# Row scales of two norms by way of DRAM, and the MLP norm's squares taken on token-major rows

## The chip, the core and the metric

One core of a Trainium2 chip runs the whole kernel. The engines are TensorE (PE, whose weight loads are listed as PEld), VectorE (DVE), ScalarE (ACT), GpSimd (POOL) and SyncE (SP, which here only issues transfers). Each engine takes its instructions in order and waits on semaphores of the others. The metric is the time of one execution in microseconds on the device.

## The reference

One layer of a streaming encoder, in float32, on 512 tokens of width 1024. Cut to what matters here:

```
def rmsnorm(x, g):
    return x * rsqrt(mean(x * x, axis=-1) + EPS) * g

hn   = rmsnorm(h, norm_mix_g);  proj = hn @ w_in        # 8 groups of columns
h    = h + concat(fox_attention, hgrn2) @ w_out
h    = h + memory_cross_attention(rmsnorm(h, norm_x_g), rmsnorm(mem, norm_mem_g))
u    = rmsnorm(h, norm_ff_g) @ w1                       # 1024 -> 4096
h    = h + square(relu(u)) @ w2                         # 4096 -> 1024
return rmsnorm(h, final_norm_g)
```

A norm's scale, one number per token, can be left out ahead of the product and put onto the product's result. The first norm's four gate columns (gf0 to gf3), its gq columns and the MLP's u are scaled this way.

## The kernel before, in words

Activations lie feature-major in SBUF for the projections: 128 features on the partitions, 512 tokens in the free dimension, eight such chunks for 1024 features. Every float32 operand is split into a high and a low part, and a product of a [128 x 512] result tile over eight chunks is 24 matmuls: high by high, high by low and low by high (lines 236 to 238, `gemm_fm`). Weights come from DRAM into raw tiles (`wr2a` and so on, 512 KB each, issued by SP), ACT copies out the high part (`wh2a`, line 171), DVE subtracts to get the low part (`wl2a`, line 175); the matmuls with the low part wait for DVE.

A feature-major result has tokens in the free dimension, so the scale must lie there too: a tile `rbc` of [128 x 512] which holds the 512 scales on every partition. The scale itself is computed with tokens on the partitions, four columns for the four blocks of 128 tokens: a [128 x 4] tile (`r0`, later `r2`). To get from the one to the other, PE multiplies each column, repeated 128 times, with the identity: four float32 matmuls of 128 columns into a PSUM bank (lines 516 and 1507), and DVE copies the bank to SBUF (lines 518 and 1508). Readers of `rbc` are the gates `sg` (line 540), the gq and fox tiles, and the MLP's `ur = max(u, 0) * rbc2` (line 1305).

Stage 1 begins the kernel. `ms0` (mean squares of x) is ready after four row sums; POOL makes r0 (lines 357 and 360). PE works on gf2 then: its broadcast is put after 15 of gf2's 24 matmuls. Chunks of x that are later needed again are parked: copied from PSUM to `xT` (`x_park`, lines 422 and 424) and written by POOL to `xTd` in DRAM. The copies also free PSUM banks, gf3's and gq's among them. In this stretch the order on ACT and DVE is the order of the code.

Stage 2 is the passage from cross-attention to the MLP. The residual's eight chunks (`xw`, in `residual`) leave PE; POOL squares each chunk and adds it into `ssq` (15 instructions of 128 x 512, lines 1073 to 1077); after the first MLP product u000, PE sums `ssq` over the partitions with a column of ones (`pm`, line 1087), DVE scales it (line 1089), POOL makes r2 and PE broadcasts it (line 1507) after u001. Meanwhile the chunks are transposed to token-major (`to_tok`), so that the rows `acc` (four tiles of [128 tokens x 1024]) collect the MLP's output. The MLP runs in eight groups of 512 hidden features: four products u(g)(j)(i) a group into two PSUM banks of the pool `mm`; `ur` and its square free the bank; then `mlp_down` multiplies in a scheme of seven products ("1", "2", "6", "5", "7", "3", "4") with banks U, Y and V. Product "6" goes into the same U bank as "1", after DVE has added "1" into `acc` (line 1335).

The raw tiles of the down weights (`wq`) are loaded by SP, and the scheme's sums of weights are made by transfers that add (`add_weights`, line 1245, issued by POOL): first from DRAM, two a group; then, once product "2" has its split, inside SBUF (`wq<-wq`: a1 += a2, then b1 += a1). The weights of product "6" are a1 after that add.

Outside stage 1 and the last product, a scheduler sets the order on each engine from the order of the code and its own estimates.

Of the kernel before, what the change touches and what calls it, by code (L numbers as in the profile page):

```python
# [42 lines left out]
def emit(  # L43
# [310 lines left out]
    def rstd_of(ms, n, name, r=None):  # L354
# [5 lines left out]
        gp.tensor_tensor(r, e, mhalf[:, 0:n], op=ALU.pow)  # L360
        return r

    def norm_rows(t, name):
        ms = sm(2, name + "m")
        for i in range(2):
            junk = t2(f"{name}j{i}")
            ac.activation(junk, t[:, i * S : (i + 1) * S], AF.Square, scale=1.0 / 32.0, accum_out=ms[:, i : i + 1])
        ve.tensor_tensor(ms[:, 0:1], ms[:, 0:1], ms[:, 1:2], ALU.add)
        r = rstd_of(ms[:, 0:1], 1, name + "r")
        ve.tensor_scalar(t, t, r, None, op0=ALU.mult)  # L370
# [67 lines left out]
    with tc.manual_schedule(engines={mybir.EngineType.Activation, mybir.EngineType.DVE}):  # L438
        ve.tensor_copy(g_mix, gmp)
        x_T(0)  # L440
        warm = mm("warm2")
        for _ in range(WARM2):
            te.matmul(warm, zero[:, 0:P], zero, start=True, stop=True)
        first[0]("v")
        x_hi(0)
        x_lo(0)
        first[0]("l")
        wt0 = stream[0]
        state["used"] = 1
        gfps = [mm(f"gf{i}") for i in range(2)]  # L450

        def first_rows(w, a, start):
            for i in range(2):
                te.matmul(gfps[i], chunk(w, 0, slice(i * P, (i + 1) * P)), a[:, 0, :], start=start, stop=False)

        first_rows(wt0[0], hn_hi, True)
        x_T(1)
        x_hi(1)
        x_lo(1)
        first_rows(wt0[0], hn_lo, False)  # L460
        first_rows(wt0[1], hn_hi, False)
        gfg = [gemm_fm(gfps[i], wt0, i * P, hn_hi, hn_lo, order=range(1, KC), begun=True) for i in range(2)]
        second = []

        def l_soft():

            gps = sc("gps", (33,))
            te.transpose(gps, rows, ident[0:33, 0:33])
            ve.tensor_copy(gv, gps)
            ve.tensor_tensor(lmx, gv[:, 25:29], gv[:, 29:33], ALU.max)  # L470
            ve.tensor_tensor(le, gv[:, 25:33].rearrange("p (r k) -> p r k", r=2), lmx.unsqueeze(1).to_broadcast([P, 2, 4]), ALU.subtract)
            ac.activation(le, le, AF.Exp)
            ve.tensor_tensor(lden, le[:, 0, :], le[:, 1, :], ALU.add)
            ve.reciprocal(lden, lden)
            ve.tensor_tensor(lb, le[:, 0, :], lden, ALU.mult)
            ve.tensor_scalar(oml, lb, -1.0, 1.0, op0=ALU.mult, op1=ALU.add)

        jobs = (
            (first[1],),
            (lambda: x_park(0), lambda: x_park(1), first[2]),  # L480
            (first[3], lambda: second.extend(load_next())),
            (lambda: x_sq(0), lambda: x_park(3)),
            (lambda: x_park(2), lambda: second[0]("h"), lambda: x_sq(2)),
            (lambda: x_sq(1), lambda: second[0]("l"), lambda: x_sq(3)),
            (lambda: second[1]("hl"), l_soft),
            (),
        )
        for c in range(KC):
            for g in gfg if c else ():
                next(g)  # L490
            if c + 2 < KC:
                x_T(c + 2)
                x_hi(c + 2)
                x_lo(c + 2)
            for job in jobs[c]:
                job()
        for g in gfg:
            assert next(g, None) is None
        x_park(7)

        wt1 = stream[1]
        state["used"] = 2
        third = load_next()
        gfps.append(mm("gf2"))
        gf2 = gemm_fm(gfps[2], wt1, 0, hn_hi, hn_lo)
        for _ in range(GF):
            next(gf2)
        r0 = cp.tile([P, NT], F32, name="r0")
        rstd_of(ms0, NT, "r0", r0)

        fb = cp.tile([P, FH], F32, name="fb")
        gp.tensor_copy(fb[:, 0:NT], r0)
        gp.dma_start(fb, fox_f_bias[0].partition_broadcast(P))
        pb = sc("rbc")
        for tb in range(NT):
            te.matmul(pb[:, tb * P : (tb + 1) * P], r0[:, tb : tb + 1].to_broadcast([P, P]), ident, start=True, stop=True)
        rbc = cp.tile([P, S], F32, name="rbc")
        ve.tensor_copy(rbc, pb)
        run_now(gf2)
        gfps.append(mm("gf3"))  # L520
        gf3 = gemm_fm(gfps[3], wt1, P, hn_hi, hn_lo)


        Fg, Mv, Sa, Ag = [], [], [], []
        for hp in range(2):
            Fg.append(s4([2, S], f"F{hp}"))
            Mv.append(s4([2, S], f"mov{hp}"))
            Sa.append(s4([2, S], f"sta{hp}"))

        def kt_(h):  # L530
            return (Sa, Mv)[h % 2][h // 2][:, h % 2, :]

        def qt_(h):
            return (Mv, Sa)[h % 2][h // 2][:, h % 2, :]


        sg = [t2(f"sg{h}") for h in range(4)]

        def gate(h):
            ve.tensor_tensor(sg[h], gfps[h], rbc, ALU.mult)  # L540
            ac.activation(sg[h], sg[h], AF.Sigmoid)

        def forget(h):
            F_ = Fg[h // 2][:, h % 2, :]
            ac.activation(F_, sg[h], AF.Identity, scale=oml[:, h : h + 1], bias=lb[:, h : h + 1])
            ac.activation(kt_(h), F_, AF.Identity, scale=-1.0, bias=1.0)

        x_park(4)
        x_park(6)
        gate(0)  # L550
        gate(1)
        x_park(5)
        third[0]()
        third[1]()
        run_now(gf3)
        gate(2)
        for h in range(3):
            forget(h)
# [3 lines left out]
    for hp in range(2):  # L562
        wt = next_panel()
        for j in range(2):
            h = 2 * hp + j
            ps = mm(f"gq{h}")
            run_now(gemm_fm(ps, wt, j * P, hn_hi, hn_lo))
            ve.tensor_tensor(qt_(h), ps, rbc, ALU.mult)
            ac.activation(qt_(h), qt_(h), AF.Silu)
# [476 lines left out]
    def residual(src_hi, src_lo, g, dst_hi, dst_lo, name, ssq, order, nlast, after=None):  # L1046
# [16 lines left out]
        def rest():  # L1063
            for c in range(KC):
                if c not in gens:
                    open_(c)
                yield from gens[c]
                hc = hTc(c)
                ve.tensor_tensor(hc, hc, ps_[c], ALU.add)  # L1069
                ac.activation(dst_hi[:, c, :], hc, AF.Identity, scale=g[:, c : c + 1])  # L1070
                ve.scalar_tensor_tensor(dst_lo[:, c, :], hc, g[:, c : c + 1], f(dst_hi[:, c, :]), op0=ALU.mult, op1=ALU.subtract)
                if c == 0:
                    gp.tensor_tensor(ssq, hc, hc, op=ALU.mult)
                else:
                    sq = t2(f"{name}sq{c}")
                    gp.tensor_tensor(sq, hc, hc, op=ALU.mult)
                    gp.tensor_tensor(ssq, ssq, sq, op=ALU.add)
                if after is not None and c in (2, 4, 6):
                    after(c - 2)
                    after(c - 1)  # L1080
# [85 lines left out]
    def to_tok(c):  # L1166
# [3 lines left out]
        for tb in range(NT):  # L1170
            d, s_ = acc[tb][:, c * P : (c + 1) * P], ps[:, tb * P : (tb + 1) * P]
            if tb % 2 == 0:
                ac.activation(d, s_, AF.Copy)
            else:
                ve.tensor_copy(d, s_)

    fill.add(x_proj(1), "xq1")
    fill.run(2.0)
    for h in range(4):
        if 0 < h < 3:  # L1180
            fill.add(x_proj(h + 1), f"xq{h + 1}")
        elif h == 3:
            x2_hi, x2_lo = act_tile("x2_hi"), act_tile("x2_lo")
            ssq2 = t2("ssq2")
            early, rest = residual(o_hi, o_lo, g_ff, x2_hi, x2_lo, "xw", ssq2, range(KC), 2, to_tok)
            fill.add(early())
        x_scores(h, 0)
        fill.run(X1)
# [107 lines left out]

    def mlp_up(g, j, wt):
        for i in range(2):
            ps = mm(f"u{g}{j}{i}")
            run_now(gemm_fm(ps, wt, i * P, x2_hi, x2_lo))  # L1300
            yield g, j, i, ps

# [171 lines left out]
    def mlp_up_group(g):  # L1474
        for j in range(2):
            if g < 2:
                wt = next_panel()
                if (g, j) == (0, 0):
                    down_raws(0)
                elif (g, j) == (1, 1):  # L1480
                    for _ in range(2):
                        unit_q.popleft()[1]()
# [14 lines left out]
    rbc2 = rbc  # L1497
    ups = mlp_up_group(0)
    up0 = next(ups)
    ms2 = mean_sq(ssq2, "pm2")  # L1500
    r2 = rstd_of(ms2, NT, "r2")
    to_tok(KC - 2)
    to_tok(KC - 1)
    up1 = next(ups)
    pb = tr("rbc2")
    for tb in range(NT):
        te.matmul(pb[:, tb * P : (tb + 1) * P], r2[:, tb : tb + 1].to_broadcast([P, P]), ident, start=True, stop=True)
    ve.tensor_copy(rbc2, pb)
    square(*up0)
    square(*up1)  # L1510
    for up in ups:
        square(*up)
    hidden_sums(0)
    for name in PRODUCTS:
# [42 lines left out]
```

## Time and profile before

| | |
|---|---|
| time, median of 3 runs | 769.85 us (768.88 to 769.93) |
| the profiled execution | 769.28 us |
| its span, first to last instruction | 767.5 us |
| PE busy | 759.0 us (99%) |
| DVE, ACT, POOL busy | 523.7 (68%), 368.7 (48%), 190.5 us (25%) |
| mean granted TensorE clock | 0.998 |
| DMA | 103.03 MB, mean 134 GB/s |

The span is 1.8 us less than the profiled execution's time; what lies around the span is the start and the end of a launch. Times on a timeline count from the span's start. A matmul's row gives its start and a duration that is modelled and reaches into the next; the distance from one start to the next is what it takes of PE. A timeline row may cover several like instructions in a row (x2, x4, x8); a float32 matmul stands as two. "Landing" is the time from a transfer's issue to its completion.

### The profile page before, as it was taken

The numbers are of one execution on the slowest core, as the hardware profiler recorded it, in microseconds if no ns is written. First come the engines' busy times: TensorE is split into PE (matmuls) and PEld (weight loads), VectorE is DVE, ScalarE is ACT, GpSimd is POOL, SyncE is SP. The second block draws the span as 40 slices with busy tenths as digits, with TensorE's granted clock in tenths as the row PEclk, the third lists the DMA queues.
The fourth block names the chain that finished last, engine by engine and source line by source line (L and its number), as shares of the span: only waits on it lengthen the run. The fifth ranks groups of instructions, "written<-read, shape, count | busy, mean of one in ns | idle before, by whom it ended". The sixth has DMA issues, their size and how long they took to land.

```text
span 767.5 us, 11244 instructions
## 1 busy us (share of the span) xinstructions
PE 759.0 (99%) x4229; PEld 646.0 (84%) x4229; DVE 523.7 (68%) x849; ACT 368.7 (48%) x620; POOL 190.5 (25%) x264
## 2 busy tenths in 40 slices
PE   9999999999999999999999999999999999999996
PEld 6889888998889988888888888888888888888885
DVE  5747765576787656555548556949596868777696
ACT  5655456665666433344444244435353535342553
POOL 7207432423432025310016510101001010101123
PEclk9999999999999999999999999999999999999999
DMA  8543332232543442231113596565748475757602
GB/s 247 192 136 108 90 84 56 80 114 57 185 149 134 163 139 83 85 100 64 56 56 108 204 262 139 146 158 175 180 149 200 139 174 161 192 137 218 138 1 109
DMA packets 79831, 103.03 MB, mean 134 GB/s; under 512 B 4593, under 2 KB 58394, under 8 KB 79778
## 3 DMA queue, kind: packets, MB, share of 16 engines
q1 hardware_dynamic: 70226, 76.61, 31.1%
q0 software_dynamic: 8960, 24.67, 15.3%
q10 hardware_dynamic: 592, 1.05, 0.4%
q8 instruction: 33, 0.54, 0.3%
q14 instruction: 20, 0.16, 0.1%
HBM read 89.71 MB, written 4.21 MB: 122 GB/s over the span
## 4 chain that ended last, share of the span: by engine, by line
PE 98%; DVE 1%; ACT 1%; POOL 0%; issue 0%; DVEq 0%; ACTq 0%
PE u L238 8%; PE u L236 8%; PE u L237 8%; PE U L1371 4%; PE U L1369 4%; PE U L1370 4%; PE xq L236 2%; PE xq L237 2%; PE xw L236 2%; PE xq L238 2%; PE xw L237 2%; PE xw L238 2%; PE wo L236 2%; PE Y L1371 2%; PE wo L238 2%; PE Y L1370 2%
## 5 line engine op out<-in xcount | busy, mean ns | idle before, releaser
L175 DVE TENSOR_TENSOR wld<-wq,whd 128x1024 fp32r<-128x1024 f32 x56 | 68.6, 1226 | 25.3 <-ACT whd L171 25.2
L236 PE MATMUL u<-x_hi,whu 128*128 128x512 f32 x192 | 74.7, 389 | 0.0
L237 PE MATMUL u<-x_lo,whu 128*128 128x512 f32 x192 | 74.7, 389 | 0.0
L238 PE MATMUL u<-x_hi,wlu 128*128 128x512 f32 x192 | 74.7, 389 | 0.0
L171 ACT ACTIVATE whd<-wq 128x1024 fp32r<-128x1024 f32 x56 | 58.4, 1054 | 30.2 <-PE u L237 18.5
L171 ACT ACTIVATE whu<-wru 128x1024 fp32r<-128x1024 f32 x24 | 25.3, 1053 | 62.1 <-DMA wru<-in_w_dram 62.1
L175 DVE TENSOR_TENSOR wlu<-wru,whu 128x1024 fp32r<-128x1024 f32 x24 | 29.5, 1229 | 32.8 <-ACT whu L171 32.8
L1245 POOL DMA_DIRECT2D wq<-in_w_dram x16 | 19.4, 1242 | 129.1 <-DMA wq<-in_w_dram 117.6
L1369 PE MATMUL U<-whd,hb 128*128 128x512 f32 x120 | 46.7, 389 | 0.0
L1370 PE MATMUL U<-wld,hb 128*128 128x512 f32 x120 | 46.7, 389 | 0.0
L1371 PE MATMUL U<-whd,hb 128*128 128x512 f32 x120 | 46.7, 389 | 0.0
L1245 POOL DMA_DIRECT2D wq<-wq x16 | 14.1, 878 | 123.9 <-DVE wld L175 96.3
L237 PEld LDWEIGHTS u<-x_lo,whu 128*128 128x128 f32 x192 | 36.0, 188 | 7.5
L238 PEld LDWEIGHTS u<-x_hi,wlu 128*128 128x128 f32 x192 | 36.0, 188 | 7.5
L236 PEld LDWEIGHTS u<-x_hi,whu 128*128 128x128 f32 x192 | 36.0, 188 | 7.4
L921 POOL TENSOR_SCALAR bi<-nF,Ft 128x128 f32<-128x128 f32 (+3 forms) x32 | 20.6, 654 | 54.6 <-PE pt L953 34.5
L1308 ACT ACTIVATE sq<-ur 128x512 f32<-128x512 f32 x32 | 20.0, 627 | 26.2 <-DVE ur L1305 26.2
L1305 DVE SCALAR_TENSOR_TENSOR ur<-u,rbc 128x512 f32<-128x512 f32 x32 | 21.9, 688 | 11.5 <-PE u L238 11.5
L1370 PEld LDWEIGHTS U<-wld,hb 128*128 128x128 f32 x120 | 22.5, 188 | 4.7
L1371 PEld LDWEIGHTS U<-whd,hb 128*128 128x128 f32 x120 | 22.5, 188 | 4.7
L1369 PEld LDWEIGHTS U<-whd,hb 128*128 128x128 f32 x120 | 22.5, 188 | 4.6
L1070 ACT ACTIVATE x_hi<-hT,gv 128x512 fp32r<-128x512 f32 x16 | 11.5, 719 | 28.5 <-DVE hT L1069 28.4
(961 smaller groups left out, 2364.2 us busy)
## 6 DMA issues: line engine op xcount, KB each, us to landing
wq<-in_w_dram SPq DMA_DIRECT2D x40, 512.0 KB, 3.3
wru<-in_w_dram SPq DMA_DIRECT2D x24, 512.0 KB, 3.8
wq<-in_w_dram POOLq DMA_DIRECT2D x16, 512.0 KB, 8.2
wq<-wq POOLq DMA_DIRECT2D x16, 512.0 KB, 4.6
xTd<-xT POOLq DMA_DIRECT2D x4, 512.0 KB, 3.3
nF<-Fd POOLq DMA_DIRECT2D x8, 256.0 KB, 3.7
hT<-xTd POOLq DMA_DIRECT2D x4, 512.0 KB, 5.4
xt<-in_x_dram SPq DMA_DIRECT2D x3, 512.0 KB
```

The lines of the kernel that those rows point to most:

```text
L171: ac.activation(hi, raw, AF.Copy)
L175: ve.tensor_tensor(lo, raw, f(hi), ALU.subtract)
L236: te.matmul(ps, wh, hi, start=n_ == 0 and not begun, stop=False)
L237: te.matmul(ps, wh, lo, start=False, stop=False)
L238: te.matmul(ps, wl, hi, start=False, stop=k == order[-1])
L921: gp.tensor_scalar(bi[:, 0:n], fF[h][:, 0:n], -1.0, Ft[:, tb, h : h + 1], op0=ALU.mult, op1=ALU.add)
L1245: gp.dma_start(raw.rearrange("p (k n) -> p k n", k=2), src, accum_op=ALU.add)
L1305: ve.scalar_tensor_tensor(u, ps, 0.0, rbc2, op0=ALU.max, op1=ALU.mult)
L1308: ac.activation(sqs[g, j][:, i, :], u, AF.Square)
L1369: te.matmul(ps, hi, whi[:, k, :], start=begin, stop=False, skip_group_check=True)
L1370: te.matmul(ps, hi, wlo[:, k, :], start=False, stop=False, skip_group_check=True)
L1371: te.matmul(ps, lo, whi[:, k, :], start=False, stop=k == 1, skip_group_check=True)
```

## The change

The two broadcasts by PE go. A function `on_all` takes their place: POOL writes the [128 x 4] tile of scales to a DRAM tile `Rd`, 16 bytes per partition, so that DRAM holds them as (partition, block); then POOL reads that row of 512 numbers (2 KB) back onto all 128 partitions (`row`, 256 KB in all), and DVE copies it into `rbc` while it puts block and partition into token order. Each of the three steps waits for the one before.

In stage 1, gf3 takes a bank of the pool `tr`, and so does gq0; the gates 0 and 1 are taken after gf3's matmuls, and all copies of `x_park` and both splits of the third panel (`third`: `wh2a`, `wl2a`, `wh2b`, `wl2b`) stand ahead of them. The write of `fb` is issued after them.

In stage 2, POOL's squares, the sum by PE and `pm2m` go. The mean squares are summed from `acc` instead: after chunk 3 is token-major ACT squares and sums columns 0 to 511 of each of the four tiles, after chunks 5 and 7 DVE squares and sums 256 columns each, four instructions each time, each with a read of the accumulator behind it. u011 and u100 take banks of the pool `sc`. `first_adds` of group 0 stands after `on_all` in the code.

```diff
--- before.py
+++ after.py
@@ -360,6 +360,15 @@
         gp.tensor_tensor(r, e, mhalf[:, 0:n], op=ALU.pow)
         return r
 
+    Rd = drp.tile([2, S], F32, name="Rd")
+
+    def on_all(i, r, dst):
+
+        gp.dma_start(Rd[i].rearrange("(p t) -> p t", t=NT), r)
+        row = t2(f"row{i}")
+        gp.dma_start(row, Rd[i].partition_broadcast(P))
+        ve.tensor_copy(dst.rearrange("p (t q) -> p t q", t=NT), row.rearrange("p (q t) -> p t q", t=NT))
+
     def norm_rows(t, name):
         ms = sm(2, name + "m")
         for i in range(2):
@@ -507,17 +516,10 @@
             next(gf2)
         r0 = cp.tile([P, NT], F32, name="r0")
         rstd_of(ms0, NT, "r0", r0)
-
-        fb = cp.tile([P, FH], F32, name="fb")
-        gp.tensor_copy(fb[:, 0:NT], r0)
-        gp.dma_start(fb, fox_f_bias[0].partition_broadcast(P))
-        pb = sc("rbc")
-        for tb in range(NT):
-            te.matmul(pb[:, tb * P : (tb + 1) * P], r0[:, tb : tb + 1].to_broadcast([P, P]), ident, start=True, stop=True)
         rbc = cp.tile([P, S], F32, name="rbc")
-        ve.tensor_copy(rbc, pb)
+        on_all(0, r0, rbc)
         run_now(gf2)
-        gfps.append(mm("gf3"))
+        gfps.append(tr("gf3"))
         gf3 = gemm_fm(gfps[3], wt1, P, hn_hi, hn_lo)
 
 
@@ -547,12 +549,16 @@
 
         x_park(4)
         x_park(6)
-        gate(0)
-        gate(1)
         x_park(5)
+
+        fb = cp.tile([P, FH], F32, name="fb")
+        gp.tensor_copy(fb[:, 0:NT], r0)
+        gp.dma_start(fb, fox_f_bias[0].partition_broadcast(P))
         third[0]()
         third[1]()
         run_now(gf3)
+        gate(0)
+        gate(1)
         gate(2)
         for h in range(3):
             forget(h)
@@ -563,7 +569,7 @@
         wt = next_panel()
         for j in range(2):
             h = 2 * hp + j
-            ps = mm(f"gq{h}")
+            ps = (mm if h else tr)(f"gq{h}")
             run_now(gemm_fm(ps, wt, j * P, hn_hi, hn_lo))
             ve.tensor_tensor(qt_(h), ps, rbc, ALU.mult)
             ac.activation(qt_(h), qt_(h), AF.Silu)
@@ -1069,7 +1075,9 @@
                 ve.tensor_tensor(hc, hc, ps_[c], ALU.add)
                 ac.activation(dst_hi[:, c, :], hc, AF.Identity, scale=g[:, c : c + 1])
                 ve.scalar_tensor_tensor(dst_lo[:, c, :], hc, g[:, c : c + 1], f(dst_hi[:, c, :]), op0=ALU.mult, op1=ALU.subtract)
-                if c == 0:
+                if ssq is None:
+                    pass
+                elif c == 0:
                     gp.tensor_tensor(ssq, hc, hc, op=ALU.mult)
                 else:
                     sq = t2(f"{name}sq{c}")
@@ -1173,6 +1181,25 @@
                 ac.activation(d, s_, AF.Copy)
             else:
                 ve.tensor_copy(d, s_)
+        if c in (3, 5, 7):
+            tok_squares(c)
+
+    ms2 = {}
+
+    def tok_squares(c):
+
+        if c == 3:
+            ms2[c] = sm(NT, "ms2")
+            for tb in range(NT):
+                ac.activation(t2(f"ms2j{tb}"), acc[tb][:, 0:S], AF.Square, scale=1.0 / 32.0, accum_out=ms2[c][:, tb : tb + 1])
+            gp.tensor_scalar(ms2[c], ms2[c], 1.0, EPS, op0=ALU.mult, op1=ALU.add)
+            return
+        cs = slice((c - 1) * P, (c + 1) * P)
+        ms2[c] = sm(NT, f"ms2{c}")
+        for tb in range(NT):
+            a, v = acc[tb][:, cs], (x[:, tb : tb + 1] for x in (ms2[c], ms2[c - 2]))
+            new_, old = v
+            ve.tensor_tensor_reduce(out=t2(f"ms2j{c}{tb}")[:, 0 : 2 * P], in0=a, in1=a, scale=1.0 / D, scalar=old, op0=ALU.mult, op1=ALU.add, accum_out=new_)
 
     fill.add(x_proj(1), "xq1")
     fill.run(2.0)
@@ -1181,8 +1208,7 @@
             fill.add(x_proj(h + 1), f"xq{h + 1}")
         elif h == 3:
             x2_hi, x2_lo = act_tile("x2_hi"), act_tile("x2_lo")
-            ssq2 = t2("ssq2")
-            early, rest = residual(o_hi, o_lo, g_ff, x2_hi, x2_lo, "xw", ssq2, range(KC), 2, to_tok)
+            early, rest = residual(o_hi, o_lo, g_ff, x2_hi, x2_lo, "xw", None, range(KC), 2, to_tok)
             fill.add(early())
         x_scores(h, 0)
         fill.run(X1)
@@ -1296,7 +1322,8 @@
 
     def mlp_up(g, j, wt):
         for i in range(2):
-            ps = mm(f"u{g}{j}{i}")
+
+            ps = (sc if (g, j, i) in ((0, 1, 1), (1, 0, 0)) else mm)(f"u{g}{j}{i}")
             run_now(gemm_fm(ps, wt, i * P, x2_hi, x2_lo))
             yield g, j, i, ps
 
@@ -1476,7 +1503,7 @@
             if g < 2:
                 wt = next_panel()
                 if (g, j) == (0, 0):
-                    down_raws(0)
+                    load_raws(0, RAWS)
                 elif (g, j) == (1, 1):
                     for _ in range(2):
                         unit_q.popleft()[1]()
@@ -1497,18 +1524,13 @@
     rbc2 = rbc
     ups = mlp_up_group(0)
     up0 = next(ups)
-    ms2 = mean_sq(ssq2, "pm2")
-    r2 = rstd_of(ms2, NT, "r2")
     to_tok(KC - 2)
     to_tok(KC - 1)
-    up1 = next(ups)
-    pb = tr("rbc2")
-    for tb in range(NT):
-        te.matmul(pb[:, tb * P : (tb + 1) * P], r2[:, tb : tb + 1].to_broadcast([P, P]), ident, start=True, stop=True)
-    ve.tensor_copy(rbc2, pb)
-    square(*up0)
-    square(*up1)
-    for up in ups:
+    r2 = sm(NT, "r2")
+    gp.tensor_tensor(r2, ms2[KC - 1], mhalf[:, 0:NT], op=ALU.pow)
+    on_all(1, r2, rbc2)
+    first_adds(0)
+    for up in [up0, *ups]:
         square(*up)
     hidden_sums(0)
     for name in PRODUCTS:
```

What stands in a row on DVE in stage 1, before. `xT` is a parked chunk, `rbc<-rbc` the copy of the broadcast out of PSUM, `sg<-gf` a gate, `wl2a` and `wl2b` the low parts of gq's first weights:

```order
COPY xT_363<-xn_327 128x512
COPY rbc<-rbc 128x512
TENSOR_TENSOR sg_419<-gf_220,rbc 128x512
TENSOR_TENSOR sg_420<-gf_221,rbc 128x512
COPY xT_423<-xn_292 128x512
TENSOR_TENSOR wl2a<-wr2a,wh2a 128x1024
TENSOR_TENSOR wl2b<-wr2b,wh2b 128x1024
```

The same place after the change:

```order
COPY xT_364<-xn_328 128x512
COPY rbc<-row_396 128x512
COPY xT_419<-xn_293 128x512
TENSOR_TENSOR wl2a<-wr2a,wh2a 128x1024
TENSOR_TENSOR wl2b<-wr2b,wh2b 128x1024
TENSOR_TENSOR sg_415<-gf_221,rbc 128x512
TENSOR_TENSOR sg_416<-gf_222,rbc 128x512
```

The copy into `rbc` keeps its place and now reads the transfer's tile; the last parked chunk and `wl2a`, which gq0 needs, stand directly behind it, and the gates behind them.

POOL at the start of the MLP, before. `xwsq` is a squared chunk, `r_4683` is r2, `wq<-in_w_dram` a load that adds:

```order
TENSOR_TENSOR xwsq_4621<-hT_3347 128x512
TENSOR_TENSOR ssq_4189<-ssq_4189,xwsq_4621 128x512
TENSOR_SCALAR r2e<-pm2m 128x4
TENSOR_TENSOR r_4683<-r2e,mhalf 128x4
DMA wq_4628<-in_w_dram 128x2x512 x2
DMA wq_4629<-in_w_dram 128x2x512 x2
DMA wq_4628<-wq_4628 128x1024
```

The same place after the change:

```order
TENSOR_SCALAR ms_4486<-ms_4486 128x4
DMA wq_4623<-in_w_dram 128x2x512 x2
TENSOR_TENSOR r_4694<-ms_4685,mhalf 128x4
DMA Rd<-r_4694 128x4
DMA row_4697<-Rd 128x512
DMA wq_4624<-in_w_dram 128x2x512 x2
DMA wq_4623<-wq_4623 128x1024
```

Group 0's two adding loads stand ahead of r2 and of the two transfers of `on_all`, group 1's behind them.

DVE at the start of the MLP, before. `wl36` and `wl37` are low parts of the weights of u01x and u10x, `hb` low parts of the hidden operands, `ur` the scaled u:

```order
TENSOR_TENSOR wl36a<-wr36a,wh36a 128x1024
COPY rbc<-rbc_4728 128x512
TENSOR_TENSOR wl36b<-wr36b,wh36b 128x1024
SCALAR_TENSOR_TENSOR ur_4734<-u_4649,rbc 128x512
SCALAR_TENSOR_TENSOR ur_4738<-u_4703,rbc 128x512
TENSOR_TENSOR hb_4818<-sq_4736,hb_4818 128x512
SCALAR_TENSOR_TENSOR ur_4778<-u_4753,rbc 128x512
TENSOR_TENSOR wl37a<-wr37a,wh37a 128x1024
SCALAR_TENSOR_TENSOR ur_4807<-u_4782,rbc 128x512
```

The same place after the change:

```order
TENSOR_TENSOR wl36a<-wr36a,wh36a 128x1024
TENSOR_TENSOR wl36b<-wr36b,wh36b 128x1024
COPY rbc<-row_4697 128x512
SCALAR_TENSOR_TENSOR ur_4789<-u_4642,rbc 128x512
SCALAR_TENSOR_TENSOR ur_4793<-u_4702,rbc 128x512
SCALAR_TENSOR_TENSOR ur_4796<-u_4739,rbc 128x512
TENSOR_TENSOR hb_4811<-sq_4791,hb_4811 128x512
TENSOR_TENSOR wl37a<-wr37a,wh37a 128x1024
SCALAR_TENSOR_TENSOR ur_4800<-u_4764,rbc 128x512
```

`wl36b` goes ahead of the copy into `rbc`, and a third `ur` stands directly behind the first two; from `wl37a` on the order is that of before, up to the first sums into `acc`: `wl37b`, ten instructions of 128 x 512 on hidden sums and `hb`, one `ur`, then `wld`, the low parts of the down weights.

## Rows read from the trace of the kernel before

**Rows 1.** The page, part 4: the chain of work that ended last, by engine.

```profile
PE 98%; DVE 1%; ACT 1%; POOL 0%; issue 0%; DVEq 0%; ACTq 0%
```

**Rows 2.** PE's waits: line, releaser, line of it: us in total, times, longest.

```profile
PE warm L348 <- DVE ones L352: 1.3, 1, 1.3
PE pst L832 <- DVE rec L853: 0.2, 1, 0.2
```

**Rows 3.** PE's timeline at 25 us: start us, us, engine, line, operation, out<-in.

```profile
24.96 1.12 PE L516 MATMUL rbc<-ident,r 128*128 128x128 f32 x8
25.84 0.47 PE L236 MATMUL gf<-hn_hi,wh1b 128*128 128x512 f32 x1
```

**Rows 4.** PE's timeline, 436 to 445 us.

```profile
436.68 0.95 PE L1087 MATMUL pm<-ones,ssq 128*128 128x1 f32 x8
437.48 0.64 PE L1169 MATMUL ht<-ident,hT 128*128 128x128 f32 x4
...
443.87 1.05 PE L1507 MATMUL rbc<-ident,r 128*128 128x128 f32 x8
444.68 0.48 PE L236 MATMUL u<-x_hi,wh35a 128*128 128x512 f32 x1
```

**Rows 5.** Timeline of POOL, 22 to 34 us.

```profile
23.79 1.08 POOL L360 TENSOR_TENSOR r<-r0e,mhalf 128x4 f32<-128x4 f32 x1
```

**Rows 6.** Last lines of the tile views of Fd, nF, fb, in order.

```profile
DMA to landing us min/median/max: 1.8/3.6/4.7
...
DMA to landing us min/median/max: 3.5/3.7/4.7
...
DMA to landing us min/median/max: 2.9/2.9/2.9
```

**Rows 7.** Timeline of DVE, 24 to 33 us.

```profile
26.12 0.69 DVE L518 COPY rbc<-rbc 128x512 f32<-128x512 f32 x1 [0.32 <-PE rbc L516]
...
29.79 1.23 DVE L175 TENSOR_TENSOR wl2a<-wr2a,wh2a 128x1024 fp32r<-128x1024 f32 x1 [1.05 <-ACT wh2a L171]
```

**Rows 8.** PE's timeline around 34 us.

```profile
33.90 0.39 PE L238 MATMUL gq<-hn_hi,wl2a 128*128 128x512 f32 x1
```

**Rows 9.** DVE's groups by line and form: busy us, mean ns, idle before.

```profile
L941 DVE CUSTOM_DVE_ANT_0 bi<-ps,bi 128x256 f32<-128x256 f32 x8 | 3.4, 422 | 5.3 <-PE ps L931 3.6 <-POOL bi L921 1.6
```

**Rows 10.** DVE's timeline, 436 to 445 us.

```profile
438.46 1.37 DVE L1175 COPY acc<-ht 128x128 f32<-128x128 f32 x4 [0.64 <-ACT acc L1173]
```

**Rows 11.** Timeline of POOL, 436 to 472 us.

```profile
439.20 2.54 POOL L1245 DMA_DIRECT2D wq<-in_w_dram  x2
...
466.43 0.89 POOL L1245 DMA_DIRECT2D wq<-wq  x1 [9.40 <-DVE wld L175]
```

**Rows 12.** The view by windows: busy by engine, PEclk, DMA share, GB/s.

```profile
433.00:454.00 21.00, 21.00 (x106) 17.74 (x105) 9.87 (x14) 6.72 (x11) 6.79 (x7) 1.00 1.07 332
```

**Rows 13.** DMA view, 438.5:442 and 443:447.6 us: queue; issues, us to landing.

```profile
q1 hardware_dynamic: 894, 1.33, 106.0%
wq<-in_w_dram POOLq DMA_DIRECT2D x2, 512.0 KB, 9.3
...
wr37a<-in_w_dram SPq DMA_DIRECT2D x1, 512.0 KB, 7.9
wr37b<-in_w_dram SPq DMA_DIRECT2D x1, 512.0 KB, 7.4
```

**Rows 14.** The page, part 6: the adds inside SBUF.

```profile
wq<-wq POOLq DMA_DIRECT2D x16, 512.0 KB, 4.6
```

**Rows 15.** DVE's timeline around 480 us.

```profile
480.25 0.69 DVE L1335 TENSOR_TENSOR acc<-U,acc 128x512 f32<-128x512 f32 x1
480.85 0.68 DVE L1315 TENSOR_TENSOR n<-s,sq 128x512 f32<-128x512 f32 x1
```

**Rows 16.** The page, part 5: ACT's pass over a weight tile.

```profile
L171 ACT ACTIVATE whd<-wq 128x1024 fp32r<-128x1024 f32 x56 | 58.4, 1054 | 30.2 <-PE u L237 18.5
```

**Rows 17.** PE's timeline around 483 us.

```profile
482.88 0.39 PE L1369 MATMUL U<-whd,hb 128*128 128x512 f32 x1
```

## The prediction

> **What bounds the kernel now.** I read the chain that ended last first: 98% of it is PE's own work, one matmul after the other [rows 1]. Then the list of what PE waits for: two lines, 1.3 and 0.2 us in 767.5, one at the start and one in a stage that the change does not touch [rows 2]. So nothing that DVE, ACT, POOL or a transfer does in the two stages concerned reaches the end of the kernel today. Two rules follow. PE work that goes is worth its full time, unless a wait takes its place. Other engines' work is worth nothing by being removed, and costs something only from the moment at which PE waits for it. The rest is therefore a search for the first matmul that would wait.
>
> **What goes from PE.** Stage 1: four float32 broadcasts start at 24.96 and the next matmul at 25.84, 0.88 us [rows 3]. Stage 2: the sum over partitions, 436.68 to 437.48, 0.80 us, and the second broadcast, 443.87 to 444.68, 0.81 us [rows 4]. Nothing is added on PE. Together 0.88 + 0.80 + 0.81 = 2.49 us, all of it on the path.
>
> POOL loses fifteen squares and sums. Since PE waits for none of them, that is worth 0; it cannot be less for lack of a cost, nor more, because there is no PE wait that it could shorten. ACT's four squares and DVE's eight reductions (0.42 us each by the nearest form [rows 9], some 4 us with their accumulator reads) lie where both engines idle more than half of the time (DVE busy 9.87 and ACT 6.72 of 21 us [rows 12]); they matter only through the moment at which r2 is ready, below.
>
> **Stage 1, the new chain.** POOL has r0 at 23.79 + 1.08 = 24.87 [rows 5]. With 0.3 us to issue, the write of 128 pieces of 16 bytes leaves at 25.2. Its landing is not in the trace; the two nearest transfers are the write of Fd to DRAM, 1.8 us (the least in its line, and less than any nF), and fb, 2.9 us, also 128 small pieces [rows 6]. I take 2.4, between the two, and keep both ends: landed at 27.6. POOL waits for that, issues the read back at 27.8, behind one parked chunk in its queue. A read of the same size and shape, nF, lands in 3.5 to 4.7 us, 3.7 in the middle [rows 6]; I take 3.8: the row is there at 31.6. From the ends, 25.1 + 1.8 + 0.1 + 3.5 = 30.5 and 25.3 + 2.9 + 0.3 + 4.7 = 33.2.
>
> DVE's copy into rbc keeps its place, and what is queued behind it is the whole point: the last parked chunk, which frees gq0's bank, then wl2a. Before, the copy was over at 26.81 and wl2a at 31.02 [rows 7]. Now copy (0.69), chunk (0.68, as the copy) and wl2a (1.23) follow the row's landing: 31.6 + 2.6 = 34.2, or 34.1 as back-to-back DVE instructions overlap a little. PE needs wl2a with gq's third matmul, at 33.90 before [rows 8] and at 33.90 - 0.88 = 33.02 now. It waits 1.1 us; the ends give 0 (row at 30.5) and 2.7. Stage 1 comes to -0.88 + 1.1 = +0.2, between -0.9 and +1.8. The strided copy itself is new; the nearest is the 0.69 above, and if it were half of that the stall would be 0.35 less. The gates move behind wl2b, but their banks are wanted a whole product later than wl2a, so I count nothing for them.
>
> By the Trainium skill, page "DMA: Bandwidth & Descriptors", section "Specifications", pieces under 512 bytes make the DMA engine read, modify and write, and so run below its line rate. That speaks for fb's 2.9 rather than Fd's 1.8 for the write of r0, and by it the sum would be 0.5 higher in this stage; no row here shows 16-byte pieces.
>
> **Stage 2, the new chain.** DVE's last copies into acc end at 438.46 + 1.37 = 439.83 [rows 10], 0.8 earlier once pm is gone; four reductions with their reads, 2 us, put the sum at about 441.0. POOL takes the power (1.08 as in stage 1) after its two adding loads, and the write of r2 leaves at about 442.5. In this stretch the DMA engines are full: a share of 1.07 from 433 to 454 us [rows 12]. What that does is in the rows: the adding loads, issued by POOL from 439.20 on [rows 11], take 9.3 us, and while they wait the only queue that moves is SP's, at 106% [rows 13]; wr37a and wr37b, issued at 443.5 and 446.8, take 7.9 and 7.4. Transfers thus land about in the order of issue. r2's write stands behind the second adding load, which lands about 10 us after its issue at 440.5, so I put it at 451. The read back is issued at 451.2, behind wr37b (446.8 + 7.4 = 454.2) and the wq load behind that (512 KB at 332 GB/s is 1.6 us: 455.8), and needs 0.8 for its own 256 KB: 456.5. Ends: 451.2 + 3.5 = 454.7 if it passes the backlog, 451.2 + 7.9 = 459.1 if it fares as wr37a did.
>
> The up products do not stall at 456.5: two more banks were given to them, and by my count the next one is wanted a little later than that. But DVE stands still for some 10 us and then has a full list in order. Counted from the row's landing: 17 instructions of 128x512 at 0.60 apart [rows 15], 10.2; wl37a, wl37b and the first wld at 1.23, 3.7; two waits for an ACT pass of 1.05 [rows 16], 2.1. The first wld ends at 16.0. Only then may POOL issue a1 += a2 (0.29 after the wld in rows 11), which lands in 4.6 [rows 14]; then ACT 1.05; then DVE's wld of product "6", a ur, another wld, a hidden sum and the sum of product "1" into acc, 1.23 + 0.60 + 1.23 + 0.60 + 0.69 = 4.35. The sum is 26.3: at 482.8 the U bank is free. Before, it was free at 480.94 [rows 15], and PE came to it at 482.88 [rows 17], with 1.9 in hand. Now PE comes at 482.88 - 1.61 = 481.3 and waits 1.5 (what stage 1 shifts, it shifts on both sides). I add 0.5 for the products right behind, since DVE has no slack there either. The wait starts when the row lands after 455.0 and then grows one for one. Stage 2 comes to -1.61 + 2.0 = +0.4, between -1.6 and 459.1 - 455.0 + 0.5 - 1.6 = +3.0.
>
> **The sum.** +0.2 and +0.4 make +0.6 on the profiled execution: 769.28 + 0.6 = 769.9. That execution lies 0.57 under the median of the three runs, within their spread; against the median it would be 770.4, so I say 770.2. A change of under 0.2%, 1.54 us, can't be told from none here.
>
> **Rivals.** (a) Both waits are covered: rows there by 30.5 and 455.0. Then the full 2.49 is kept: 766.8 on the profiled execution, 767.4 on the median. For it: the short landings are in the trace, and each threshold is within a microsecond of my estimate. Against it: both must come out at their good end, and the second behind full queues. A variant, one covered and one not, gives -0.5 to -1.4 and is still within 0.2%.
>
> (b) Queues share. If the DMA engines served POOL's queue and SP's in turns, r2's two small transfers would pass SP's backlog; the row would be there at 454.7 or before, and stage 2 would keep its 1.6: 769.28 + 0.2 - 1.6 = 767.9. Against it: in 438.5 to 442 SP's queue alone moved, with POOL's loads already issued [rows 13]. By the Trainium skill, the same page, section "Queues, rings and completion order", each DMA engine takes turns between its queues, a packet at a time; here the 106% of one queue is against it.
>
> (c) Slower: the second row lands late. If it fares as wr37a (459.1), DVE's list begins 2.6 later and product "6" waits 4.1 instead of 1.5, and u101 waits a little for its bank: 769.28 + 0.2 + 3.0 = 772.5, and 773 to 774 with stage 1 at its long end. It decides from a landing of about 457.6. For it: nothing in the trace is as dependent as a read behind a write, both through full queues. Against it: the stretch of full DMA engines ends soon after 454, and SP's next loads wait for DVE, which itself waits for the row.
>
> **Chances.** The forecast, +0.6, with both waits of about a microsecond: 0.45; (a) 0.13; (b) 0.15; (c) 0.27. (a) is faster by over 0.2%, and of (b) a third; (c) is slower by over 0.2%, with a little of the forecast's upper side. So faster 0.18, same 0.5, slower 0.32. The range goes from (a)'s 767.2 to 772.8 in (c); the forecast's own is 768.8 to 771.5.
>
> **What would show it.** PE's list of waits after: right if gq's matmul of wl2a (or the gq bank's chunk copy) waits about 1 us for DVE, and a U matmul of product "6" about 1.5 us for DVE's sum into acc; rows' landings at 31.6 and 456.5; r2's write landing some 8 us after its issue. Wrong, step by step: no wait at gq means the two transfers of stage 1 took under 5.3 us together; no wait at "6" with a row after 455 means that DVE's list was shorter than I count; a wait of an up product instead means that the bank is the limit, not the sum; r2's write landing in 2 to 3 us while wr37a is under way means that queues share.

## The result, and the profile after

The changed kernel takes 770.57 us in the median of 22 runs (769.62 to 771.84), the kernel before 769.42 in as many (768.87 to 769.93): a ratio of 1.0014 with a 95% interval of 1.0009 to 1.0020. That is 1.15 us more (0.7 to 1.5), 0.14%. The forecast was +0.6 us, said as 770.2.

PE's list of waits has four new lines. First its view, in us in total, times, longest (line numbers move from kernel to kernel: U's wait is L1396 here and L1399 in some of the experiments):

```profile
PE gq L236 <- DVE xT L433: 1.1, 1, 1.1
PE U L1396 <- DVE acc L1362: 1.1, 1, 1.1
PE gq L238 <- DVE wl2a L175: 0.3, 1, 0.3
PE U L1396 <- DVE acc L1364: 0.2, 1, 0.2
```

Of the two waits in [rows 2] nothing has changed. The new ones lie where the prediction put them: gq's first product in stage 1, and the U bank in stage 2.

PE in stage 1, the changed kernel; the matmuls that answer to [rows 3, 8]:

```profile
24.09 0.39 PE L238 MATMUL gf<-hn_hi,wl1b 128*128 128x512 f32 x1
24.32 0.39 PE L236 MATMUL gf<-hn_hi,wh1b 128*128 128x512 f32 x1
...
31.57 0.39 PE L238 MATMUL gf<-hn_hi,wl1b 128*128 128x512 f32 x1
33.10 0.47 PE L236 MATMUL gq<-hn_hi,wh2a 128*128 128x512 f32 x1 [1.15 <-DVE xT L433]
...
34.15 0.50 PE L238 MATMUL gq<-hn_hi,wl2a 128*128 128x512 f32 x1 [0.34 <-DVE wl2a L175]
34.48 0.39 PE L236 MATMUL gq<-hn_hi,wh2a 128*128 128x512 f32 x1
```

Where the broadcast stood, the next matmul now follows after 0.23 us (24.09 to 24.32). gq begins at 33.10 after a gap from 31.57, and its third matmul, with wl2a, waits once more.

What released them, POOL first and then DVE, answering to [rows 5, 7]:

```profile
23.12 1.08 POOL L360 TENSOR_TENSOR r<-r0e,mhalf 128x4 f32<-128x4 f32 x1
24.50 0.63 POOL L367 DMA_DIRECT2D Rd<-r  x1 [0.29 <-POOL r L360]
...
27.25 0.55 POOL L369 DMA_DIRECT2D row<-Rd  x1 [0.52 <-DMA Rd<-r]
```

```profile
31.74 0.62 DVE L370 COPY rbc<-row 128x512 f32<-128x512 f32 x1 [6.61 <-DMA row<-Rd]
32.27 0.68 DVE L433 COPY xT<-xn 128x512 f32<-128x512 f32 x1
32.88 1.22 DVE L175 TENSOR_TENSOR wl2a<-wr2a,wh2a 128x1024 fp32r<-128x1024 f32 x1
```

And the landing times of the tiles Rd and row (the last lines of their views; both stages in one line, so least and most are one stage each):

```profile
DMA to landing us min/median/max: 2.5/4.5/9.3
...
DMA to landing us min/median/max: 4.5/4.5/4.6
```

r0 is ready at 24.20, its write lands 2.5 us after 24.50, the row 4.5 us after 27.25. The copy into rbc starts at 31.74, and behind it stand the parked chunk that frees gq0's bank, over at 32.95, and wl2a, over at 34.10. PE starts at 33.10 and 34.15.

Stage 2, PE, answering to [rows 4, 17]:

```profile
437.06 0.60 PE L1177 MATMUL ht<-ident,hT 128*128 128x128 f32 x4
...
443.16 0.39 PE L238 MATMUL u<-x_hi,wl34b 128*128 128x512 f32 x1
443.38 0.39 PE L236 MATMUL u<-x_hi,wh35a 128*128 128x512 f32 x1
...
481.24 0.39 PE L1398 MATMUL V<-whd,hb 128*128 128x512 f32 x1
482.75 0.47 PE L1396 MATMUL U<-whd,hb 128*128 128x512 f32 x1 [1.12 <-DVE acc L1362]
```

Both other pieces are gone: 443.16 to 443.38 has nothing between. Product "6" starts at 482.75, 1.5 us after the matmul before it. POOL and DVE there, answering to [rows 11, 15]:

```profile
438.61 2.55 POOL L1271 DMA_DIRECT2D wq<-in_w_dram  x2 [19.85 <-DVE acc L1183]
...
442.52 0.64 POOL L367 DMA_DIRECT2D Rd<-r  x1 [0.30 <-POOL r L1530]
452.11 0.57 POOL L369 DMA_DIRECT2D row<-Rd  x1 [8.95 <-DMA Rd<-r]
...
472.75 0.88 POOL L1271 DMA_DIRECT2D wq<-wq  x1 [15.18 <-DVE wld L175]
```

```profile
456.70 0.73 DVE L370 COPY rbc<-row 128x512 f32<-128x512 f32 x1 [10.69 <-DMA row<-Rd]
...
471.22 1.22 DVE L175 TENSOR_TENSOR wld<-wq,whd 128x1024 fp32r<-128x1024 f32 x1
...
478.44 1.23 DVE L175 TENSOR_TENSOR wld<-wq,whd 128x1024 fp32r<-128x1024 f32 x1 [2.74 <-ACT whd L171]
...
481.91 0.69 DVE L1362 TENSOR_TENSOR acc<-U,acc 128x512 f32<-128x512 f32 x1
```

r2's write takes 9.3 us from 442.52, the row 4.6 from 452.11. From the copy at 456.70 to the end of the first wld (472.44) DVE has 15.7 us of list; the sum that frees the U bank ends at 482.60.

**Where the time went, by PE's starts.** I subtract the start of the same matmul before from that after, and take the steps. Stage 1 saves 0.97 (0.88, and 0.09 in the first matmul behind the broadcast, 0.32 to the next start before and 0.22 after) and loses 1.97 (1.31 at gq's first matmul, 0.51 at its third, the rest in slower first steps behind each wait): +1.00. Stage 2 saves 1.70 (0.80, 0.81, 0.09) and loses 2.20 (1.28 at product "6", 0.39 at product "7", 0.5 in smaller steps up to 494 us): +0.50. Together +1.50. The profiled spans differ by only 0.7, because the changed kernel's profiled execution was 0.65 quicker over its first six microseconds, in code that is the same (at 5 us PE's transposes start 0.11 us apart there and 0.21 before): gf's first matmul starts at 5.97 there, at 6.62 before, and at 5.96 to 6.88 in the nine profiles below. I take that as a difference between executions; the medians (+1.15) lie between. How much of the 0.35 between +1.50 and +1.15 it explains is not shown, as there is one profile of each kernel.

### The profile page after: what moved, and what is told of

The parts are those of the page before. It is cut to its first block, busy times and chain, and to the rows that moved or that the text cites. A ratio compares the mean times of both kernels' runs of the same rounds, so it can differ in the third digit from the quotient of the medians.

```text
span 768.2 us, 11198 instructions
## 1 busy us (share of the span) xinstructions
PE 757.1 (99%) x4205; PEld 642.4 (84%) x4205; DVE 517.8 (67%) x864; ACT 370.9 (48%) x628; POOL 170.1 (22%) x253
## 4 chain that ended last, share of the span: by engine, by line
PE 89%; issue 3%; DMA 3%; DVE 2%; ACT 1%; POOL 1%; SPq 0%; DVEq 0%; POOLq 0%; ACTq 0%
PE u L237 6%; PE u L236 6%; PE u L238 6%; PE U L1396 3%; PE U L1397 3%; PE U L1398 3%; PE xq L236 2%; PE xq L237 2%; PE xw L236 2%; PE xq L238 2%; PE xw L237 2%; PE xw L238 2%; PE wo L236 2%; PE wo L238 2%; PE wo L237 2%
## 5 line engine op out<-in xcount | busy, mean ns | idle before, releaser
L1396 PE MATMUL U<-whd,hb 128*128 128x512 f32 x120 | 46.9, 391 | 1.4 <-DVE acc L1362 1.1
L1396 PEld LDWEIGHTS U<-whd,hb 128*128 128x128 f32 x120 | 22.5, 188 | 7.1 <-ACT whd L171 1.5
L1352 ACT ACTIVATE hb<-s 128x512 fp32r<-128x512 f32 x24 | 15.1, 631 | 20.9 <-PE U L1398 13.9
```

Source lines behind the costliest of these rows:

```text
L1396: te.matmul(ps, hi, whi[:, k, :], start=begin, stop=False, skip_group_check=True)
```

## The experiments

**e1: the copy into rbc behind the splits.**

```diff
-        on_all(0, r0, rbc)            # with its copy, ahead of x_park(5) and third
+        # write and read here, the copy later:
         third[1]()
+        ve.tensor_copy(rbc..., row0...)
```

> The changed kernel, with one edit: in stage 1 DVE copies the row into rbc after the last parked chunk and after wl2a and wl2b instead of ahead of them; transfers, banks and stage 2 stay. Theory A (the stall is DVE's order: a copy that waits for the row stands ahead of what gq0 needs): no PE wait at gq0, where the changed kernel lost 1.31 + 0.08 + 0.51 + 0.11 = 2.0 us; the row still lands at about 31.7 to 32.4 us, and only the gates wait for it; time 770.57 - 2.0 = 768.6. Rival B (the stall is the banks: gq0 in another pool, gates late): gq0 waits still, or the wait moves to gq1 or gq2, whose banks the gates free; at least 1 us of wait remains and the time stays at 769.6 or more.

Measured: 768.83 us, ratio to before 0.9997 (0.9988 to 1.0005); 1.74 less than the changed kernel's 770.57. DVE in stage 1, and PE's new waits:

```profile
25.93 1.23 DVE L175 TENSOR_TENSOR wl2a<-wr2a,wh2a 128x1024 fp32r<-128x1024 f32 x1
28.23 1.23 DVE L175 TENSOR_TENSOR wl2b<-wr2b,wh2b 128x1024 fp32r<-128x1024 f32 x1 [1.07 <-ACT wh2b L171]
33.80 0.62 DVE L561 COPY rbc<-row 128x512 f32<-128x512 f32 x1 [4.33 <-DMA row<-Rd]
```

```profile
PE U L1399 <- DVE acc L1365: 0.9, 1, 0.9
PE dg L638 <- DVE z L614: 0.6, 1, 0.6
```

The waits at gq are gone, so theory A holds: it was DVE's order. Rival B's banks are not the limit. Two things I had not expected. The row lands two microseconds later than in the changed kernel, 6.3 us after its issue at 27.48: wl2a, now done at 27.2, frees its raw tile and lets the next weight load go, just ahead of the row. And the late gates bring a new wait of 0.64 for z at 60 us (0.8 with the step behind it). Stage 1 then saves 0.97 and loses 0.81.

**e2 and e3: each stage alone.** The diff is the shown one, cut to the hunks of one stage.

> Only stage 1 of the change (row of r0 by way of DRAM, banks and order of the gates); stage 2 is that of the kernel before. Theory A (both stages lose, each by its own wait): PE saves 0.97 and waits 2.0 at gq0, +1.0 against before: 770.5, no wait at the U bank. Rival C (all of the loss is stage 2's, and stage 1's wait is made up later): 769.42 - 1.0 = 768.5.

> Only stage 2 of the change; stage 1 is that of the kernel before. Theory A: PE saves 0.80 + 0.81 + 0.09 = 1.70 and waits about 2.3 (products 6 and after, for DVE's sums), +0.6 against before: 770.0. The second row lands at about 456 to 457 us. Rival C (all of the loss is stage 2's): +1.15, 770.6.

Measured: e2 770.40, ratio 1.0015 (1.0006 to 1.0024); e3 770.77, ratio 1.0020 (1.0011 to 1.0028). Waits of PE, e2 and then e3:

```profile
PE gq L236 <- DVE xT L433: 1.1, 1, 1.1
PE gq L238 <- DVE wl2a L175: 0.3, 1, 0.3
```

```profile
PE U L1399 <- DVE acc L1365: 1.8, 1, 1.8
```

e2 is as theory A said: +1.1, with the waits of the changed kernel. e3 is +1.5, beyond A's +0.6 and nearer to C's +1.15, but not for C's reason, since stage 1 alone loses too. Its profile shows two things. The row lands 5.5 us after its issue instead of 4.6, and PE waits 1.8 instead of 1.1. And then PE runs slowly: e3's PE behind that wait, and the busy time, granted clock (third number from the end), DMA share and GB/s of 485 to 487 us:

```profile
483.14 0.47 PE L1399 MATMUL U<-whd,hb 128*128 128x512 f32 x1 [1.83 <-DVE acc L1365]
...
484.56 0.63 PE L1401 MATMUL U<-whd,hb 128*128 128x512 f32 x1
484.99 0.63 PE L1399 MATMUL U<-whd,hb 128*128 128x512 f32 x1
```

```profile
485.00:487.00 2.00, 2.00 (x6) 1.62 (x5) 2.00 (x4) 0.26 (x1) 0.00 (x0) 0.50 0.97 360
```

Starts are 0.43 apart instead of 0.23, at a granted clock of 0.50, the lower of the two levels (1.2 GHz). Over eight matmuls that is 1.6 us more. e3's eleven runs spread from 769.18 at a mean clock of 0.999 to 772.33 at 0.996, so it seems that not every execution has it. The parts thus do not add up to the whole (1.1 + 1.5 against 1.15); why the row lands a microsecond later in e3 than in the changed kernel I did not find out.

**e4: r2 written from ACT's queue.**

```diff
-    on_all(1, r2, rbc2)
+    ac.dma_start(Rd[1]..., r2)        # then read and copied as in on_all
```

> The changed kernel, with one edit: the write of r2 to DRAM is issued by ACT instead of POOL, so in another queue than the adding loads; the read back stays with POOL. Theory D (the DMA engines serve what was issued in about the order of issue, whichever queue): the write lands 8 to 9 us after its issue as before, at about 451, the row at about 456; time as the changed kernel, 770.6. Rival E (order holds inside a queue only, queues take turns): the write lands in 2 to 3 us, at about 445, the row is read from 445.5 on and lands at 449 to 450; no wait at product 6; 770.57 - 2.3 = 768.3.

Measured: 768.81, ratio 0.9994 (0.9985 to 1.0003); 1.76 less than the changed kernel. The tile view of Rd, its transfers in stage 2 and the landings, and POOL's timeline at the read:

```profile
L1531 ACTq DMA_DIRECT2D Rd<-r x1: 362/362/362, 442.4 to 442.4; - x1
L1533 POOL DMA_DIRECT2D row<-Rd x1: 633/633/633, 448.6 to 448.6; - x1
...
DMA to landing us min/median/max: 2.6/4.2/5.6
```

```profile
448.56 0.63 POOL L1533 DMA_DIRECT2D row<-Rd  x1 [6.24 <-DMA Rd<-r]
```

The three landings are stage 1's write, stage 1's row and stage 2's row; ACT's write has none in this view. POOL's read, which waits for it, is issued at 448.56, and in the other runs such a read is issued 0.3 us after the write has landed; so the write landed at about 448.3. By this estimate it takes 5.9 us instead of 9.3; the row takes another 5.6, and the copy starts at 454.17. No U wait is left, and stage 2 keeps its 1.70 whole. Neither theory has it right: the write does not pass everything in 2 to 3 us (E), but it does pass POOL's second adding load (issued at 439.8, landed at 451.2), and so the order of issue does not hold over all queues (D). Nearer to E.

**The threshold.** With PE's first ht transposes as zero, the second row's copy starts at 19.64 in the changed kernel, 20.49 in e3, 19.50 in e1, 16.97 in e4. Product "6" would start at 44.50 without a wait (45.40 in [rows 4, 17], less 0.90); it starts 1.19, 1.90, 1.01 and 0 later. Row less wait is 18.45, 18.59 and 18.49: one for one, from 18.5 on. The prediction's 455.0 was 18.3 on this scale.

**e5: loads held until r2.**

```diff
-                    load_raws(0, RAWS)             # at the start of the MLP
+                    load_raws(0, RAWS[0:1])
 ...
+    for i in range(1, 8):
+        gp.tensor_copy(slots[i][:, 0:1], r2[:, 0:1])   # ahead of the loads into them
     on_all(1, r2, rbc2)
+    load_raws(0, RAWS[1:])
```

> The changed kernel, with one edit: seven of the first eight loads of down weights are held back until r2 is there (POOL writes one column of r2 into each of their tiles first, which the load overwrites), so that the DMA engines are nearly empty when r2 is written. Theory F (what makes the two transfers slow is the loads ahead of them): the write lands in about 3 us, before 446, the row in 4 to 5, before 451; no wait at product 6; 770.57 - 2.3 = 768.3. Rival G (a write to DRAM and a read behind it are slow in themselves): still 5 us or more each, row at 453 or later. Rival H: the held loads are late themselves, PE waits at products 1, 2 or 5 for the split of their weights, and the time is 769.5 or more.

Measured: 771.48, ratio 1.0023 (1.0014 to 1.0032). The edit missed its aim: the held loads were let go at 445.1, 0.6 ahead of the write, and ran beside it. Write 5.7 us, row 6.5, the wait at "6" as in the changed kernel. It tells nothing of empty engines; e10 repeats it. But it shows one thing beside e4: here the write is in POOL's queue again, with SP's loads beside it and no adding load ahead of it (they are issued at 452.2), and takes 5.7 us, not 9.3.

**e7: stage 1's row alone in its queue.** As e1 and e4 together, and:

```diff
-            gp.dma_start(xTd[part], park[part])        # parts 3 and 2
+            ac.dma_start(xTd[part], park[part])        # behind third
```

> The copy behind the splits as in e1, the write of r2 by ACT as in e4, and the two last parked chunks written by ACT instead of POOL, so that the row of r0 is alone in POOL's queue. Theory A with queues in turns: row of r0 lands 3.7 to 4.5 us after its issue (31.2 to 32 against 33.8 in e1), the gates begin 2 us earlier, PE's wait of 0.64 us for z at 60 us goes; both stages keep all that PE saved, 0.97 + 1.70: 769.3 - 2.67 = 766.7. Rival: the row is slow because of all the loads of that stretch, not because of its queue; it lands at 33 or later, the wait for z stays: 767.5.

Measured: 767.58, ratio 0.9974 (0.9964 to 0.9984). The rival was right about the row: 6.7 us, slower than in any other kernel's stage 1, the copy at 35.07. Taking the parked chunks out of its queue did not help; their writes are still issued beside the row, at 28.0 and 28.5 us, from ACT's. Waits for weights (0.4 with the step behind it) and for z (0.5) cost about 0.9 us; stage 2's 1.70 is what this kernel gains.

**e8: only the squares.** The kernel before, with the token-major squares and both broadcasts on PE.

> The kernel before, with only the squares changed: mean squares from the token-major rows on ACT and DVE, no squares on POOL, no sum over partitions on PE; both broadcasts stay on PE. Theory A: pm's 0.80 us goes from PE and nothing takes its place, since r2 is ready by 442.2 and PE comes to its broadcast at 443.1: 769.3 - 0.8 = 768.5. Rival: r2 is late for the broadcast, or DVE's eight reductions push the low parts behind them; PE waits there and the time is 769.1 or more.

Measured: 768.50, ratio 0.9985 (0.9976 to 0.9993), no new wait of PE. By PE's starts the gain is 0.80, pm's time, and nothing takes its place.

**e9: the next loads later.** As e1 and e4 together, and:

```diff
-        third[0]()
         third[1]()
+        third[0]()
```

> As e1 (copy behind the splits) with r2 written by ACT as in e4, and in stage 1 the second half of the third panel split before the first (wl2b, then wl2a), so that the loads wr3a and wr3b, which need the tiles that these two free, are issued at about 29.4 and 30.6 us instead of 27.2 and 29.5, two microseconds or more behind the row's issue. Theory I (the row of r0 is slow, 4.5 us in the changed kernel and 6.3 to 6.7 in e1 and e7, because of the weight loads that are issued next to it): it lands 4 us after its issue, by 31.7 us, the gates begin by 32.3, no wait at gq0 nor for z; both stages keep what PE saved, 0.97 + 1.70: 769.4 - 2.67 = 766.8. Rival J (the two parked chunks' writes slow it, not the loads): it lands after 33 as in e1, the wait for z stays at about 0.8: 767.6. A wait at gq0 for wl2a of up to 0.5 would mean that the swap itself is late.

Measured: 766.95, ratio 0.9969 (0.9958 to 0.9980), the fastest of all. PE's whole list of waits, and DVE in stage 1:

```profile
PE warm L348 <- DVE ones L352: 1.3, 1, 1.3
PE pst L841 <- DVE rec L862: 0.2, 1, 0.2
```

```profile
28.89 1.23 DVE L175 TENSOR_TENSOR wl2b<-wr2b,wh2b 128x1024 fp32r<-128x1024 f32 x1 [2.38 <-ACT wh2b L171]
30.03 1.22 DVE L175 TENSOR_TENSOR wl2a<-wr2a,wh2a 128x1024 fp32r<-128x1024 f32 x1
32.87 0.62 DVE L561 COPY rbc<-row 128x512 f32<-128x512 f32 x1 [1.62 <-DMA row<-Rd]
```

PE keeps the full 0.97 + 1.70 = 2.67 us. The row lands 4.7 us after its issue at 28.18, against 6.3 and 6.7 where wr3a is issued 0.3 and 0.6 ahead of it (here 2.0 behind it): theory I, though a microsecond later than it said. The parked chunks are written by POOL around the row as in e1, so rival J is out. The row is soon enough for z.

**e10: loads held until the row.** As e5, with `row1[:, 0:1]` for `r2[:, 0:1]` and behind the read.

> The changed kernel with the same seven loads held as in e5, but until the row of r2 has landed (POOL writes a column of the row into each of their tiles first, which the load overwrites). In e5 they were let go 0.6 us ahead of the write of r2 and ran beside it, so that it showed nothing of empty engines. Theory F: with only wr36b, wr37a and wr37b about, the write lands in 2.5 to 3 us, the row in 4 to 5, at about 450; the wait at product 6 goes, unless the held loads and adds are late for it; 768.3. Rival G: two dependent transfers are slow in themselves: 5 us or more each, row at 453 or later. Rival H: row at 450, but the held loads miss products 2, 6 or 5: PE waits for a split of weights there, 769.5 or more.

Measured: 773.41, ratio 1.0062 (1.0047 to 1.0078). The profiled execution is the slowest of six, 777.22 (the others 772.89 to 774.97). POOL's two transfers, the landing of Rd's tile, and PE's wait at the U bank:

```profile
444.69 0.62 POOL L1531 DMA_DIRECT2D Rd<-r  x1 [0.29 <-POOL r L1530]
446.74 0.55 POOL L1533 DMA_DIRECT2D row<-Rd  x1 [1.43 <-DMA Rd<-r]
...
DMA to landing us min/median/max: 1.8/3.5/6.5
```

```profile
PE U L1396 <- DVE acc L1362: 4.8, 1, 4.8
```

With empty engines the same write lands in 1.8 us, not 9.3: theory F for the write, and G is out for it. The row takes 6.5 us, with wr37a and wr37b issued at 445.6 and 448.3; stage 1's rows of 4.2 to 4.7 us, with no weight load issued within 4 us of them, speak against G there. And rival H for the time: the held loads, and with them a1 += a2, are late, and PE waits 4.8 us at "6".

## Why the prediction was right

**What PE saves.** Predicted 2.49; measured 2.67. The 0.18 are the two first matmuls behind a broadcast, which the sum left out.

**Stage 1.** Right in kind: PE waits for DVE's list behind a copy that waits for a transfer (e1 takes the waits away without touching a transfer). Too small: +0.2 against +1.00. The terms up to the row's issue hold: r0 to issue 0.30 us, write 2.5 against 2.4. The term that was mis-sized is the read, taken as 3.8 from nF's middle and in fact 4.5. It was inside the stated ends (3.5 to 4.7). That the row is there at 31.7, as forecast (31.6), is luck: this execution runs 0.65 ahead of the one before, on whose timeline the row would stand at 32.4. nF's rows came from a stretch with other neighbours, and e1, e7 and e9 show what moves this number: 6.3 and 6.7 us with a weight load issued just ahead of the row, 4.5 and 4.7 with none issued within 1.9 us of it. Also left out: gq's first matmul waits for the parked chunk before the third waits for wl2a, and each restart costs some 0.1 in slow first steps.

**Stage 2.** Right in place and nearly in size: +0.4 against +0.50. Write issued at 442.5 (442.52 measured), landed at 451 (451.8), row landed at 456.5 (456.7), first wld over 16.0 later (15.7), bank free 26.3 later (25.9). The product's wait was 1.5 in the sum and is 1.1 to 1.3; the follow-up, 0.5 in the sum, is 0.9. Part of this is luck: the write took 9.3 us where the sum had 8.5, and the read 4.6 where it had 5.3, and the two errors cancel in the row's landing.

**The order of issue.** The argument for 451 was that transfers land in about that order. The trace after agrees, but e4 shows that the reason was narrower: the write stood behind two adding loads in its own queue. In another queue it is 3.4 us quicker among the same loads; in e5, in POOL's queue but with no adding load ahead of it, it is 3.6 quicker. So rival (b) was dismissed too firmly. The Trainium skill, page "DMA: Bandwidth & Descriptors", section "Queues, rings and completion order", has each DMA engine take turns between its queues. The trace of e4 agrees in part: the write, issued at 442.35, lands ahead of POOL's second load, but none of its packets moves before 446 us, while SP's and POOL's queues do. Why it waits that long for its turn stays open.

**What was open.** The Trainium skill, the same page, section "Specifications", has pieces under 512 bytes go below the line rate. The prediction put that at 0.5 in stage 1. The 128 pieces of 16 bytes took 2.5 us there, 0.1 above the sum's 2.4, and 1.8 with empty engines in e10, as much as Fd's rows [rows 6]. No cost of the small pieces is seen.

## What to carry to other kernels

A row that goes through DRAM is two dependent transfers, and its price is set by what else is in flight: here 1.8 to 9.3 us for the same 2 KB written. When such a transfer replaces PE's work, the copy that waits for it must stand last on its engine among what PE needs next; put it there, give the transfer a queue without bulk loads, and see that what you finish early does not let the next bulk load go beside it. Those three moves turn +1.15 us into -2.3 here. The queue counted in stage 2 alone, where bulk loads stood in POOL's (e4); in stage 1, emptying it did not make the row quicker (e7). And 0.80 of the 2.67 us that e9 saves on PE come from the squares, without any row (e8).

## What the runs showed of the hardware

At some waits PE's clock fell. In e3 (a wait of 1.8 us) and in e10 (4.8), the matmuls behind ran at the lower level; e10, busy times, granted clock, DMA share and GB/s:

```profile
489.00:493.00 4.00, 4.00 (x10) 3.13 (x11) 4.00 (x8) 1.58 (x2) 0.00 (x0) 0.50 0.75 259
```

At 0.50 a matmul takes 0.2 us more, in e3 1.6 us in all. In e5 and e10 the same is seen in gq, behind waits of 1.3 and 1.2 us (each with one of 0.3 close behind), and costs some 1.6 us each time, in a stage that their edits do not touch. In the profiled executions of the changed kernel and of e2, waits of 1.1 us, also with 0.3 behind, were not followed by it. So a wait can cost more than its length; which waits do it, these runs don't settle.
